# S5's rotation table built per group of four, with priority for the gates' weight splits and the late adaLN steps behind S5's steps

## The chip, the core and the metric

One core of a Trainium2 chip. The metric is the device time of one execution in microseconds (us), as the median of the runs shown. The engines are TensorE (PE, matmuls), VectorE (DVE), ScalarE (ACT), GpSimd (POOL) and SyncE (SP), whose queue issues most DMAs.

## The reference, cut to what matters

```python
mod = jax.nn.silu(c) @ w_ada + b_ada                       # six vectors of 1024
h = layer_norm(x) * (1.0 + scale1) + shift1                # 1024 x 1024
z = h @ w_in
zq, zkv, zg, zs, zm = jnp.split(z, splits, axis=-1)        # zm: 2048 columns, zs: 512
o_a = nsa_attention(...)                                   # from zq, zkv, zg
y_s = s5_ssm(zs, ...)                                      # 32 groups x 64 states, complex
zz = jax.nn.gelu(y_s) @ w_s5_glu
y_b = zz[..., :d] * jax.nn.sigmoid(zz[..., d:])
g_a, g_b = jnp.split(zm, 2, axis=-1)
mix = (jax.nn.sigmoid(g_a) * (o_a @ w_nsa_out) + jax.nn.sigmoid(g_b) * y_b) @ w_o
x = layer_norm(alpha * x + gate1 * mix) * ln1_g + ln1_b    # then a gated MLP with a conv
```

The S5 mixer is a scan over 1024 positions with the state multiplied by a complex number at each step. The kernel cuts the sequence into 128 blocks of 8 positions. Between blocks it needs the complex rotation e^(i·angle·c) for c = 0 to 127: this is the table E, which is built by doubling (the first n columns times the rotation of n blocks give the next n).

## The kernel before

Order of the stages: layer norm of x and the first two adaLN vectors; the S5 input `zs` (matmuls `pz`) and S5's parameters (`s5_params`); then sixteen gates `zm` of 128 columns each with S5 beside them; then keys, values and queries, attention, the merge and the MLP. Each weight is split into a high and a low part, and a product is three matmuls (`mm3`: high·high, low·high, high·low).

**A gate** (`z_gate`, zm0 to zm15) is 48 matmuls of 128x512. Its weight comes through the class `Stream`: a DMA on SP loads `wr` (512 KB, three buffers), ACT makes `wh` from it (L112), DVE (POOL from the tenth gate on) the remainder `wl` (L113). The first matmul of a gate needs `wh`, the third `wl`. `wl` frees the `wr` buffer for a later load.

**Late adaLN steps.** After each gate stand two steps (`late`, `ada_acc`) that add one more 128 rows of w_ada, scaled, to an accumulator `acc` (DVE L263 for the first, L265 for the others). They take `wr` buffers from the same three, so SP's queue holds in turn one gate weight and two such loads, in order. I call the steps l0, l1, l2 and so on: l0 and l1 belong to zm0.

**S5** (`s5_steps`, a generator) goes through four groups of four states, q4 = 0 to 3, in three pieces each, one piece for each `next(s5)`, which stands at the end of `z_gate`:
- POOL makes the products `s5V` and `s5W` of the group (14 instructions, L589 to L608), DVE copies `s5V` into `s5VB` (L617);
- PE makes `s5pk`, `s5pu`, `s5pw` (8 matmuls each), DVE and ACT write them out; `s5kt` goes to memory and comes back as `s5T`;
- PE makes `s5pb`, ACT copies it to `s5B`, and DVE runs a chain of 27 instructions on it and on E: six on `s5r` (L668 to L673), eight scans `s5S` (L677), four multiplications (L681 to L684) and four that give `s5X` (L688, L689). PE's `s5py` needs `s5X`.

Engines work in order; a scheduler fixes the order from the program's order and priorities. E of before is built in `s5_params` in two halves of eight states, with its real and imaginary part in separate tiles; the first half lies in the tile `bias`, which the attention's bias needs later (L906 to L911 on POOL write it).

Of the kernel before, what the change touches and what calls it, by code (L numbers as in the profile page):

```python
# [33 lines left out]
def kernel(  # L34
# [6 lines left out]
    V, A, G, TE, SP = nc.vector, nc.scalar, nc.gpsimd, nc.tensor, nc.sync  # L41
# [12 lines left out]
    def Bt(shape, dt=F32, name="b"):  # L54
        return sp.tile(shape, dt, name=name, tag="B", bufs=20)
# [13 lines left out]
    bc = lambda a, shape: a.to_broadcast(list(shape))  # L69


    class Stream:
# [20 lines left out]
        def split(self, upto):  # L93
            while self.ns < min(upto, len(self.specs)):
                i = self.ns
                _, shape, eng, dest, raw_only, scale = self.specs[i]
                self.load(i + 1)
                r = self.raw.pop(i)
                self.ns += 1
                if raw_only:  # L100
                    self.hl[i] = r
                    continue
                if callable(dest):
                    h, l = dest()
                elif dest is None:
                    h = sp.tile([P] + list(shape), F32R, name="wh", tag="wh", bufs=2)
                    l = sp.tile([P] + list(shape), F32R, name="wl", tag="wl", bufs=2)
                else:
                    h, l = Bt([P] + list(shape), F32R, "bh"), Bt([P] + list(shape), F32R, "bl")
                if scale is not None:  # L110
                    (V if eng is G else G).tensor_mul(r, r, self.scales[scale])  # L111
                A.activation(h, r, AF.Copy)  # L112
                (eng or G).tensor_sub(l, r, h.bitcast(F32))  # L113
                self.hl[i] = (h, l)

        def get(self, i, ahead=3, split=2):
# [2 lines left out]
            self.split(i + split)  # L119
            return self.hl.pop(i)  # L120

    W = Stream()

    def colw(w, ncols, c0, n, k0=0, nk=8):
        return ap(w, k0 * P * ncols + c0, [ncols, P], [P * ncols, nk], [1, n])
# [16 lines left out]
    for i in range(NT):  # L142
        t = (Bt if i < 4 else Ct)([P, 1024], name="x")
# [23 lines left out]
    ORDER = [("z", m) for m in range(16)] + [(t[0], int(t[1])) for t in "r0 r1 k0 c0 k1 c1 q0 C0 q1 C1 q2 n0 q3 n1".split()]  # L167
    for kind, n in ORDER:
        if kind == "z":
            zm_i[n] = W.add([(None, colw(w_in, IN_COLS, C_ZM + P * n, P))], [8, P], eng=V if n < 10 else G)  # L170
            for v, k in lateada[2 * n:2 * n + 2]:
                late_i[v, k] = W.add([(None, ada_src(v, k))], [1024], raw_only=True)
        elif kind == "r":
            kc_i[n] = W.add([(None, colw(w_in, IN_COLS, (C_KC, C_VC)[n], P))], [8, P], eng=V)
        elif kind == "n":
            for kk, (k0, nk) in enumerate(((0, 3), (3, 3), (6, 2))):
                nat_i[n, kk] = W.add([((slice(None), slice(0, nk), slice(0, 128)), colw(w_in, IN_COLS, C_VS, 128, k0, nk)),
                                      ((slice(None), slice(0, nk), slice(128, 280)), colw(w_in, IN_COLS, C_VW, 152, k0, nk))],
                                     [nk, 280], eng=V)
# [182 lines left out]
    bias_t = lambda: sp.tile([P, 2176], F32, name="bias", tag="bias", bufs=1)  # L362

    def s5_params():
# [9 lines left out]
        bbt = Bt([P, 4, 16, 16], name="s5bb")  # L374
# [7 lines left out]
        p = ps(name="s5p")  # L382
        TE.transpose(p[:, 0:36], rows2, ident[0:36, 0:36])
        prm = cst.tile([P, 36], F32, name="s5prm")
        V.tensor_copy(prm, p[:, 0:36])
        p = ps(name="s5c")
# [3 lines left out]
        CT = Bt([P, 3, 16, 16], name="s5CT")  # L390
# [34 lines left out]
        cs, sn = tab[:, 320:480], tab[:, 480:640]  # L425
        nn, q, z, r2, a1, a2 = (wk[:, k] for k in range(6))
# [39 lines left out]
        for d, n in ((2, 1), (4, 3)):  # L466
            br, bi = (bc(L[:, a, d:d + 1], [P, n, 16]) for a in range(2))
# [6 lines left out]
        LT = Bt([P, 2, 16, 17], name="s5LT")  # L474
        for a in range(2):
            V.tensor_copy(LT[:, a, :, 0:9], L[:, a].rearrange("p d q -> p q d"))
            for j in range(8):
# [24 lines left out]
        G.tensor_tensor(tmp, bbt[:, 2], cib, op=OP.mult)  # L502
        G.tensor_tensor(bbt[:, 1], bbt[:, 1], tmp, op=OP.add)

        et = bias_t()
        E = [[et[:, 1024 * a:1024 * a + 1024].rearrange("p (q c) -> p q c", q=8) for a in range(2)],
             [Bt([P, 8, 128], name="s5E") for _ in range(2)]]
        for qh in range(2):
            er, ei = E[qh]
            V.memset(er[:, :, 0:1], 1.0)  # L510
            V.memset(ei[:, :, 0:1], 0.0)
            u1 = Bt([P, 8, 64], name="s5u1")
            u2 = Bt([P, 8, 64], name="s5u2")
            for k in range(7):
                n = 1 << k
                c0 = 16 * (3 + k) + 8 * qh
                br, bi = (bc(t[:, c0:c0 + 8][:, :, None], [P, 8, n]) for t in (cs, sn))
                V.tensor_tensor(u1[:, :, :n], er[:, :, 0:n], br, op=OP.mult)
                V.tensor_tensor(u2[:, :, :n], ei[:, :, 0:n], bi, op=OP.mult)
                V.tensor_tensor(er[:, :, n:2 * n], u1[:, :, :n], u2[:, :, :n], op=OP.subtract)  # L520
                V.tensor_tensor(u1[:, :, :n], er[:, :, 0:n], bi, op=OP.mult)
                V.tensor_tensor(u2[:, :, :n], ei[:, :, 0:n], br, op=OP.mult)
                V.tensor_tensor(ei[:, :, n:2 * n], u1[:, :, :n], u2[:, :, :n], op=OP.add)
        BZ = Bt([P, 2, 4, P], name="s5BZ")
        G.memset(BZ, 0.0)
        VB = Bt([P, 2, 4, P], name="s5VB")
# [3 lines left out]
            V.tensor_add(dmask, dmask, ident[:, 16 * m:16 * m + 16])  # L530
        m8 = cst.tile([P, 16], F32, name="s5m8")
        V.tensor_copy(m8, mg[:, 48:64])
        return dict(CT=CT, LT=LT, bb=bbt, E=E, BZ=BZ, VB=VB, m8=m8, dmask=dmask, Dc=prm[:, 32:36])

    kd_d = dp.tile([32, 16, 240], F32, name="kd_d")
    ys_d = dp.tile([P, 4, 1024], F32, name="ys_d")
# [45 lines left out]
    def s5_steps():  # L582
        S = S5
        for q4 in range(4):
# [30 lines left out]
            for a in range(2):  # L615
                for g2 in range(2):
                    V.tensor_copy(S["VB"][64 * a:64 * a + 64, g2], Vt[a][64 * g2:64 * g2 + 64].rearrange("p s d h -> p s (d h)"))  # L617
            yield
            pk = ps((P, P), name="s5pk")
            n = 0  # L620
# [38 lines left out]
            for g2 in range(2):  # L659
                for a in range(2):  # L660
                    A.activation(Bv[64 * g2:64 * g2 + 64, a],
                                 pb[g2][64 * a:64 * a + 64].rearrange("p (s c) -> p s c", s=4), AF.Copy)
            e0, e1 = (t[:, q0 % 8:q0 % 8 + 4] for t in S["E"][q4 // 2])
            N1 = slice(0, 127)
            N2 = slice(1, 128)
            r0 = Bt([P, 2, 4, P], name="s5r0")
# [71 lines left out]
    def z_gate(m):  # L738
        wh, wl = W.get(zm_i[m])
        p = mm("zm")  # L740
        gemmT(p, wh, wl, hH, hL, KD)
        sg = Bt([P, 1024], name="sg")
        A.activation(sg, p, AF.Tanh, scale=0.5)
        A.dma_start(zm_d[m], sg)
        for v, k in lateada[2 * m:2 * m + 2]:
            late(v, k)
        next(s5, None)


    vcs = cst.tile([P, 2, P], F32R, name="vcs")  # L750
# [854 lines left out]
```

## Time and profile before

| what | value |
|---|---|
| runs | 1692.97, 1693.41, 1701.58 us; median 1693.41 us |
| the profiled execution | 1698.03 us, its span 1696.3 us |
| PE busy in the span | 1569.0 us (92%) |
| DVE, POOL, ACT busy | 1239.6, 706.2, 691.1 us |
| TensorE clock granted, mean | 0.969 |
| first matmul of zm0 / zm2 / zm3 / zm8 | 97.1 / 123.4 / 152.7 / 232.9 us |

Times within the rows are microseconds from the start of the span. The busy time of an engine says how full it is over the whole span; what a stage costs is read from the idle time of PE in that stage, which is shown in square brackets together with what ended it.

### The profile page before, as it was taken

The page shows a single profiled execution, that of the slowest core. Times are in us where ns is not written, and L with a number is a line of the kernel's source. Part 1 is how long each engine was busy: PE and PEld are TensorE (multiplying, and loading weights), DVE is VectorE, ACT ScalarE, POOL GpSimd, SP SyncE. Part 2 cuts the span into 40 slices and gives each one's busy share as a digit, 9 for nine tenths or more (in the row PEclk, how much of TensorE's full clock was granted, in tenths as well). Part 3 has the DMA queues.
Part 4 walks back from the last instruction along what each step waited for, and adds up shares of the span by engine and source line. Part 5 has one row for each costly group of instructions (what it writes and reads, how often), then busy time and mean ns, then how long its engine had stood idle before and what let it go on. Part 6 is the DMA issues. An engine that isn't in the chain of part 4 may idle for free.

```text
span 1696.3 us, 21512 instructions
## 1 busy us (share of the span) xinstructions
PE 1569.0 (92%) x7707; PEld 1304.0 (77%) x7707; DVE 1239.6 (73%) x2263; ACT 691.1 (41%) x1303; POOL 706.2 (42%) x584
## 2 busy tenths in 40 slices
PE   6987899999999999999998579999999998899996
PEld 4976787878989999788787357777777776688885
DVE  8699766565399999553658876888888888855448
ACT  4423223224399999421323433444344333311101
POOL 4342355400066566222536634544444555521105
PEclk8998999999999999999999789999999999999998
DMA  9235544622200010443411112222222227522102
GB/s 341 70 113 151 167 146 152 202 64 79 71 20 1 14 38 2 145 132 123 137 62 63 38 50 87 75 75 75 75 75 75 75 88 251 208 100 99 39 2 99
DMA packets 150128, 164.36 MB, mean 97 GB/s; under 512 B 20633, under 2 KB 123777, under 8 KB 150021
## 3 DMA queue, kind: packets, MB, share of 16 engines
q1 hardware_dynamic: 146357, 151.74, 27.9%
q10 hardware_dynamic: 3664, 11.24, 1.7%
q8 instruction: 61, 1.00, 0.2%
q14 instruction: 46, 0.38, 0.1%
HBM read 132.04 MB, written 30.91 MB: 96 GB/s over the span
## 4 chain that ended last, share of the span: by engine, by line
PE 57%; DVE 27%; issue 6%; ACT 5%; POOL 2%; DMA 2%; SPq 0%; DVEq 0%; ACTq 0%; POOLq 0%
DVE cv L1382 5%; PE dn L1472 4%; PE dn L1474 4%; PE dn L1473 4%; PE oacc L1008 3%; PE pT L1019 3%; PE up L1346 3%; PE up L1348 2%; PE up L1347 2%; DVE us L1321 2%; PE zm L128 2%; PE zm L130 2%; ACT cv L1379 2%; PE zm L129 2%; DVE us L1306 2%
## 5 line engine op out<-in xcount | busy, mean ns | idle before, releaser
L982 POOL TENSOR_SCALAR Pm<-Pm,gate,fc 128x64 f32<-128x64 f32 (+4 forms) x192 | 123.8, 659 | 57.3 <-DVE fc L980 56.8
L1472 PE MATMUL dn<-dnh,fh 128*128 128x512 f32 x320 | 124.9, 390 | 4.5 <-DVE facc L1570 4.5
L1296 POOL TENSOR_TENSOR ul<-wr,uh 128x512 fp32r<-128x512 f32 x44 | 77.7, 1785 | 115.4 <-ACT uh L1295 115.4
L1474 PE MATMUL dn<-dnh,fl 128*128 128x512 f32 x320 | 124.1, 389 | 1.6 <-DVE fl L1463 1.6
L1570 DVE SCALAR_TENSOR_TENSOR facc<-facc,dn 128x512 f32<-128x512 f32 x96 | 64.7, 681 | 83.3 <-PE dn L1474 83.3
L1473 PE MATMUL dn<-dnl,fh 128*128 128x512 f32 x320 | 124.5, 389 | 0.0
L978 ACT ACTIVATE Pm<-Pm,ng 128x64 f32<-128x64 f32 (+6 forms) x192 | 114.7, 602 | 6.5 <-DVE ng L959 5.0
L130 PE MATMUL zm<-hTh,wl 128*128 128x512 f32 x256 | 101.8, 398 | 13.1 <-DVE wl L113 13.1
L112 ACT ACTIVATE wh<-wr 128x1024 fp32r<-128x1024 f32 (+3 forms) x59 | 57.7, 978 | 137.8 <-PE ya L129 30.6
L111 POOL TENSOR_TENSOR wr<-wr,g2b 128x1024 f32<-128x1024 f32 x22 | 63.3, 2885 | 120.5 <-DMA wr<-in_w_down_dram 79.4
L1023 DVE TENSOR_TENSOR Pt<-pT,Pt 128x512 fp32r<-128x512 f32 (+1 forms) x160 | 100.6, 642 | 9.7 <-ACT Pt L1022 8.7
L128 PE MATMUL zm<-hTh,wh 128*128 128x512 f32 x256 | 101.9, 398 | 2.9 <-ACT wh L112 2.5
L1008 PE MATMUL oacc<-Pt,Vs 128*128 128x256 f32 x528 | 102.6, 304 | 0.9 <-DVE Pt L1023 0.4
L129 PE MATMUL zm<-hTl,wh 128*128 128x512 f32 x256 | 101.2, 395 | 0.0
L113 DVE TENSOR_TENSOR wl<-wr,wh 128x1024 fp32r<-128x1024 f32 (+2 forms) x40 | 51.8, 1294 | 64.4 <-ACT wh L112 64.2
L1019 PE MATMUL pT<-ident,Pm 128*128 128x128 f32 x592 | 91.3, 273 | 1.9 <-DVE yl L1082 1.0
L1379 ACT ACTIVATE cv<-u,cw 128x512 f32<-128x512 f32 x44 | 35.6, 809 | 140.3 <-DVE u L1369 132.7
L1022 ACT ACTIVATE Pt<-pT 128x512 fp32r<-128x512 f32 (+1 forms) x160 | 87.4, 560 | 13.1 <-PE pT L1019 12.1
L1382 DVE SCALAR_TENSOR_TENSOR cv<-u,cw,cv 128x511 f32<-128x511 f32 x88 | 74.8, 851 | 19.7 <-ACT cv L1379 18.8
L1347 PE MATMUL up<-h2b,uh 128*128 128x512 f32 (+1 forms) x184 | 72.2, 393 | 15.1 <-POOL h2b L1199 15.1
L1346 PE MATMUL up<-h2b,uh 128*128 128x512 f32 (+1 forms) x184 | 74.4, 406 | 12.1 <-DVE bias L1355 9.0
L1323 POOL TENSOR_TENSOR ul<-us,uh 128x1024 fp32r<-128x1024 f32 x22 | 52.8, 2398 | 74.8 <-ACT uh L1322 71.2
(507 smaller groups left out, 4871.0 us busy)
## 6 DMA issues: line engine op xcount, KB each, us to landing
wr<-in_w_up_dram SPq DMA_DIRECT2D x44, 512.0 KB, 3.8
wr<-in_w_in_dram SPq DMA_DIRECT2D x32, 512.0 KB, 4.2
wr<-in_w_ada_dram SPq DMA_DIRECT2D x32, 512.0 KB, 4.1
ff_d<-cv SPq DMA_DIRECT2D x22, 512.0 KB, 2.8
wr<-in_w_down_dram SPq DMA_DIRECT2D x22, 512.0 KB, 4.0
fl<-ff_d SPq DMA_DIRECT2D x22, 512.0 KB, 6.0
ar<-in_w_ada_dram SPq DMA_DIRECT2D x16, 512.0 KB, 9.4
zm_d<-sg ACTq DMA_DIRECT2D x16, 512.0 KB, 2.9
```

The costliest lines, as they stand in the source:

```text
L128: TE.matmul(po, wh, rh, start=start, stop=False, skip_group_check=skip)
L129: TE.matmul(po, wh, rl, start=False, stop=False, skip_group_check=skip)
L130: TE.matmul(po, wl, rh, start=False, stop=stop, skip_group_check=skip)
L978: A.activation(Pm[ii][:, c0:c0 + n], Pm[ii][:, c0:c0 + n], AF.Exp, bias=ng[:, ii, br:br + 1], scale=-1.0, accum_out=dn[:, ii, br:br + 1])
L982: G.tensor_scalar(Pm[ii][:, c0:c0 + n], Pm[ii][:, c0:c0 + n], gate[:, i, 3 * h + br:3 * h + br + 1], fc[:, ii, br:br + 1], op0=OP.mult, op ...
L1008: TE.matmul(acc[:, a0:a0 + 256], vt, ptile[:, hl, 256 * w:256 * w + 256], start=(first and n == 1), stop=(last and n == nmm), skip_group_c ...
L1019: TE.transpose(p[:, o:o + P], Pm[e][:, c0:c0 + P], ident)
L1346: TE.matmul(po, wh[:, q], h, start=(q == 0 and j not in (3, 4, 7)), stop=False, skip_group_check=True)
L1382: V.scalar_tensor_tensor(dst[:, c0:c0 + n], src[:, 0:n], tap(d), dst[:, c0:c0 + n], op0=OP.mult, op1=OP.add)
L1472: TE.matmul(p, ff[0][:, c0], wd[0][:, s], start=(e == 0), stop=False)
L1473: TE.matmul(p, ff[0][:, c0], wd[1][:, s], start=False, stop=False)
L1474: TE.matmul(p, ff[1][:, c0], wd[0][:, s], start=False, stop=(e == len(fs) - 1))
```

## The change

E is built by `make_E(q4)` once for each group of four, from within that group's first piece of `s5_steps`. Real and imaginary part lie in one tile, so that one multiplication takes both with the cosine and one both with the sine: four instructions per doubling instead of six per half of eight. `bias` is no longer used for it. The split of a gate's weight (`wh`, `wl`) runs under the scheduler's high priority. In `z_gate` the S5 piece is now ahead of the two late steps.

```diff
@@ Stream.split
-                A.activation(h, r, AF.Copy)
-                (eng or G).tensor_sub(l, r, h.bitcast(F32))
+                with tc.high_priority() if i in urgent else ExitStack():
+                    A.activation(h, r, AF.Copy)
+                    (eng or G).tensor_sub(l, r, h.bitcast(F32))
@@ ORDER, for a gate
+            urgent.add(len(W.specs))
             zm_i[n] = W.add(...)
@@ s5_params
-        et = bias_t()
-        E = [[et[:, 1024 * a:1024 * a + 1024].rearrange("p (q c) -> p q c", q=8) for a in range(2)],
-             [Bt([P, 8, 128], name="s5E") for _ in range(2)]]
-        for qh in range(2):
-            er, ei = E[qh]
-            V.memset(er[:, :, 0:1], 1.0)
-            V.memset(ei[:, :, 0:1], 0.0)
-            u1 = Bt([P, 8, 64], name="s5u1")
-            u2 = Bt([P, 8, 64], name="s5u2")
+        def make_E(q4):
+            t = Bt([P, 2, 4, 128], name="s5E")
+            V.memset(t[:, 0, :, 0:1], 1.0)
+            V.memset(t[:, 1, :, 0:1], 0.0)
+            uu = Bt([P, 2, 2, 4, 64], name="s5u")
             for k in range(7):
                 n = 1 << k
-                c0 = 16 * (3 + k) + 8 * qh
-                br, bi = (bc(t[:, c0:c0 + 8][:, :, None], [P, 8, n]) for t in (cs, sn))
-                V.tensor_tensor(u1[:, :, :n], er[:, :, 0:n], br, op=OP.mult)
-                V.tensor_tensor(u2[:, :, :n], ei[:, :, 0:n], bi, op=OP.mult)
-                V.tensor_tensor(er[:, :, n:2 * n], u1[:, :, :n], u2[:, :, :n], op=OP.subtract)
-                V.tensor_tensor(u1[:, :, :n], er[:, :, 0:n], bi, op=OP.mult)
-                V.tensor_tensor(u2[:, :, :n], ei[:, :, 0:n], br, op=OP.mult)
-                V.tensor_tensor(ei[:, :, n:2 * n], u1[:, :, :n], u2[:, :, :n], op=OP.add)
+                c0 = 16 * (3 + k) + 4 * q4
+                for i, a in enumerate((cs, sn)):
+                    V.tensor_tensor(uu[:, i, :, :, :n], t[:, :, :, 0:n], bc(a[:, None, c0:c0 + 4, None], [P, 2, 4, n]),
+                                    op=OP.mult)
+                V.tensor_tensor(t[:, 0, :, n:2 * n], uu[:, 0, 0, :, :n], uu[:, 1, 1, :, :n], op=OP.subtract)
+                V.tensor_tensor(t[:, 1, :, n:2 * n], uu[:, 1, 0, :, :n], uu[:, 0, 1, :, :n], op=OP.add)
+            return t
@@ s5_steps, after the copies into s5VB
+            E = S["make_E"](q4)
             yield
@@ z_gate
+        next(s5, None)
         for v, k in lateada[2 * m:2 * m + 2]:
             late(v, k)
-        next(s5, None)
```

What the scheduler makes of it stands in the order of the instructions. Lines of the changed kernel are three higher from L263 on (L263 becomes L266, L265 becomes L268) and one higher from about L500 on. First DVE, from the last S5 parameters on, with zm1 running on PE. Before:

```order
L518 TENSOR_TENSOR s5u_787<-bias,s5tab 128x8
L519 TENSOR_TENSOR s5u_788<-bias,s5tab 128x8
L510 MEMSET s5E 128x8
L511 MEMSET s5E 128x8
L520 TENSOR_TENSOR bias<-s5u_787,s5u_788 128x8
L518 TENSOR_TENSOR s5u_833<-s5E,s5tab 128x8
L519 TENSOR_TENSOR s5u_834<-s5E,s5tab 128x8
L263 TENSOR_SCALAR acc<-wr,scol 128x1024
```

and after the change, at the same place:

```order
L617 COPY s5VB<-s5V 64x512 x2
L511 MEMSET s5E 128x4
L512 MEMSET s5E 128x4
L518 TENSOR_TENSOR s5u<-s5E,s5tab 128x8 x2
L266 TENSOR_SCALAR acc<-wr,scol 128x1024
L520 TENSOR_TENSOR s5E<-s5u 128x4
L521 TENSOR_TENSOR s5E<-s5u 128x4
L628 MEMSET s5kt 128x112
L268 SCALAR_TENSOR_TENSOR acc<-wr,scol,acc 128x1024
```

The first pair of copies into `s5VB`, which stood some fifty rows further down, is now ahead of E's first instructions and of l0 (L266) and l1 (the first L268).

PE, from the end of zm1 on. Before, zm2 begins at once (its first rows are not shown), and S5's products of q4 = 0 are strewn over its 48 matmuls; this is where they begin:

```order
L128 MATMUL zm<-hTh,wh 128x512
L623 MATMUL s5pk<-s5V,s5BZ 128x128
L641 MATMUL s5pu<-ident,uc 128x128 x8
L129 MATMUL zm<-hTl,wh 128x512
L130 MATMUL zm<-hTh,wl 128x512
L128 MATMUL zm<-hTh,wh 128x512
L129 MATMUL zm<-hTl,wh 128x512
L623 MATMUL s5pk<-s5V,s5BZ 128x128 x7
```

After, from the last matmul of zm1 to the first of zm2:

```order
L132 MATMUL zm<-hTh,wl 128x512
L624 MATMUL s5pk<-s5V,s5BZ 128x128
L642 MATMUL s5pu<-ident,uc 128x128 x8
L624 MATMUL s5pk<-s5V,s5BZ 128x128 x7
L649 MATMUL s5pw<-ident,s5W 128x2x64 x8
L130 MATMUL zm<-hTh,wh 128x512
```

All 24 products of q4 = 0 now stand between zm1 and zm2. In the same way q4 = 0's `s5pb` stands ahead of zm3 (before: seven matmuls into it), and all its `s5py` ahead of zm4 (before: after 42 of zm4's matmuls).

POOL, between the products of q4 = 1 and of q4 = 2. Before:

```order
L608 TENSOR_TENSOR s5W<-s5W,s5tA 128x512
L906 IOTA bias 128x1024
L907 IOTA bias 128x640
L908 IOTA bias 128x512
L910 TENSOR_SCALAR bias<-bias 128x2176
L911 AFFINE_SELECT bias<-bias 128x1024
L911 AFFINE_SELECT bias<-bias 128x640
L911 AFFINE_SELECT bias<-bias 128x512
L911 AFFINE_SELECT bias<-bias 128x640
L589 COPY s5V<-s5CT 128x4x16
L590 TENSOR_SCALAR s5V<-s5CT 128x4x16
```

After:

```order
L608 TENSOR_TENSOR s5W<-s5W,s5tA 128x512
L589 COPY s5V<-s5CT 128x4x16
L590 TENSOR_SCALAR s5V<-s5CT 128x4x16
L594 TENSOR_TENSOR s5V<-s5CT,s5LT 128x4x128
```

The eight instructions that prepare the attention's bias have left this place; they now stand at the start of the program, right behind the identity matrix and ahead of POOL's share of the layer norm of x.

## Rows read from the trace of the kernel before

**Rows 1.** PE, idle between zm2 and zm5: start, duration, instruction, idle before it and what ended it.

```profile
123.42 0.50 PE L128 MATMUL zm<-hTh,wh 128*128 128x512 f32 x1 [2.48 <-ACT wh L112]
...
135.81 0.79 PE L130 MATMUL zm<-hTh,wl 128*128 128x512 f32 x1 [11.66 <-DVE wl L113]
...
184.80 0.80 PE L701 MATMUL s5py<-s5VB,s5X 128*128 128x128 f32 x2 [7.47 <-DVE s5X L689]
```

**Rows 2.** Windows of PE: stretch, length, busy (instructions), granted clock, DMA share, GB/s.

```profile
110.00:120.00 10.00, 10.00 (x46) 1.00 0.37 119
135.80:142.00 6.20, 6.19 (x20) 0.53 0.76 187
185.00:192.00 7.00, 7.00 (x36) 0.69 0.59 179
```

**Rows 3.** DVE beside zm1's end and zm2: start, duration, instruction.

```profile
114.40 1.13 DVE L263 TENSOR_SCALAR acc<-wr,scol 128x1024 f32<-128x1024 f32 x1
...
115.77 2.17 DVE L265 SCALAR_TENSOR_TENSOR acc<-wr,scol,acc 128x1024 f32<-128x1024 f32 x1
117.86 1.03 DVE L523 TENSOR_TENSOR bias<-s5u,s5u 128x8 f32<-128x8 f32 x1
...
137.28 0.84 DVE L617 COPY s5VB<-s5V 64x512 f32<-64x512 f32 x2
```

**Rows 4.** DVE at the start of the program.

```profile
3.53 0.58 DVE L530 TENSOR_TENSOR s5dm<-s5dm,ident 128x16 f32<-128x16 f32 x3
5.59 1.29 DVE L240 BATCH_NORM_STATS2 bn<-x 128x6 f32<-128x512 f32 x2 [1.47 <-DMA x<-in_x_dram]
```

**Rows 5.** POOL, products of q4 = 0.

```profile
116.82 2.04 POOL L595 TENSOR_TENSOR s5tA<-s5CT,s5LT 128x512 f32<-128x512 f32 x1
118.82 1.07 POOL L597 TENSOR_TENSOR s5V<-s5CT,s5LT 128x512 f32<-128x512 f32 x1
...
123.48 1.27 POOL L596 TENSOR_TENSOR s5V<-s5V,s5tA 128x512 f32<-128x512 f32 x1
...
132.58 1.30 POOL L608 TENSOR_TENSOR s5W<-s5W,s5tA 128x512 f32<-128x512 f32 x1
```

**Rows 6.** SP, the issue of zm2's load.

```profile
117.97 0.38 SPq L89 DMA_DIRECT2D wr<-in_w_in_dram  x1
```

**Rows 7.** ACT, zm2's wh.

```profile
122.31 1.06 ACT L112 ACTIVATE wh<-wr 128x1024 fp32r<-128x1024 f32 x1 [5.50 <-DMA wr<-in_w_in_dram]
```

**Rows 8.** DVE's chain of q4 = 1, then PE's first product with its s5X.

```profile
221.31 0.69 DVE L668 TENSOR_TENSOR s5r<-s5B,bias 128x508 f32<-128x508 f32 x1 [2.00 <-ACT s5B L661]
...
224.90 1.69 DVE L677 TENSOR_TENSOR_SCAN s5S<-s5m,s5r 128x127 f32<-128x127 f32 x5
...
231.22 1.40 DVE L689 TENSOR_TENSOR s5X<-s5r 64x508 f32<-64x508 f32 x2
...
231.96 0.49 PE L701 MATMUL s5py<-s5VB,s5X 128*128 128x128 f32 x2
```

**Rows 9.** DVE's chain of q4 = 0 from the scans on, then POOL's first product of q4 = 1.

```profile
165.80 3.31 DVE L677 TENSOR_TENSOR_SCAN s5S<-s5m,s5r 128x127 f32<-128x127 f32 x5
...
174.73 2.08 DVE L113 TENSOR_TENSOR wl<-wr,wh 128x1024 fp32r<-128x1024 f32 x1
...
183.12 2.35 DVE L689 TENSOR_TENSOR s5X<-s5r 64x508 f32<-64x508 f32 x2
...
164.74 1.50 POOL L589 COPY s5V<-s5CT 128x64 f32<-128x64 f32 x1 [30.86 <-DVE s5E L523]
```

**Rows 10.** POOL, the preparation of bias, then the products of q4 = 2.

```profile
229.98 0.98 POOL L906 IOTA bias<- 128x1024 f32 x1 [45.77 <-DVE s5r L683]
...
232.22 2.28 POOL L910 TENSOR_SCALAR bias<-bias 128x2176 f32<-128x2176 f32 x1
234.57 5.29 POOL L911 TENSOR_SCALAR_AFFINE_SELECT bias<-bias 128x1024 f32<-128x1024 f32 x4
239.82 1.21 POOL L589 COPY s5V<-s5CT 128x64 f32<-128x64 f32 x1
```

More of the change, by code (lines that the diff above doesn't have):

```diff
@@ L120, in get @@
             return self.hl.pop(i)
+    urgent = set()
     W = Stream()
@@ L532, in s5_params @@
         V.tensor_copy(m8, mg[:, 48:64])
-        return dict(CT=CT, LT=LT, bb=bbt, E=E, BZ=BZ, VB=VB, m8=m8, dmask=dmask, Dc=prm[:, 32:36])
+        return dict(CT=CT, LT=LT, bb=bbt, make_E=make_E, BZ=BZ, VB=VB, m8=m8, dmask=dmask, Dc=prm[:, 32:36])
     kd_d = dp.tile([32, 16, 240], F32, name="kd_d")
@@ L662, in s5_steps @@
                                  pb[g2][64 * a:64 * a + 64].rearrange("p (s c) -> p s c", s=4), AF.Copy)
-            e0, e1 = (t[:, q0 % 8:q0 % 8 + 4] for t in S["E"][q4 // 2])
+            e0, e1 = E[:, 0], E[:, 1]
             N1 = slice(0, 127)
```

## The prediction

> **What bounds the kernel now.** The table of busy times comes first: PE has by far the most work, so time is won or lost where PE stands still or runs at its lower clock. I then went through PE's own rows for idle time in the stretch that the change touches, from zm0 to the end of the gates. Three places hold nearly all of it [rows 1]. zm2 starts after 2.48 us without work, because its `wh` was late; two matmuls on, PE waits 11.66 us for `wl`; and in zm4 it waits 7.47 us for `s5X` of q4 = 0. The reader should then look at the windows [rows 2]: behind the first two waits PE works 6.20 us at a granted clock of 0.53, behind the third 7.00 us at 0.69, against 1.00 beside zm1. [...] So 21.6 us of waits and 5.1 us of clock are there to be won, 26.7 us or 1.6% of 1693 us. Everything else from zm0 on is PE at work, so whatever the change wins or loses here goes through to the end nearly one to one.
>
> Why is `wl` of zm2 late? DVE's rows of that time [rows 3] show one instruction of 8 elements that takes 1.03 us, where three of 16 elements took 0.58 us together at the start [rows 4]: POOL is at its products then, and DVE's small instructions wait for it. `wl` stands behind E's instructions in DVE's order. Priority for `wl` removes that. The question is what PE waits for next.
>
> **zm2 (one term).** DVE's order after the change puts the first copies into `s5VB` ahead of E and of l0 and l1. These copies need POOL's L596, which in the trace ends at 123.48 + 1.27 = 124.75 [rows 5]. DVE is through with the parameters just ahead of l0's 114.40, so it now stands still for some nine us. POOL has the time for itself: a product that took 2.04 us takes 1.07 us alone [rows 5], two such are found ahead of L596, and I take 122.8 for its end. Then come the copies (0.84 us), four small instructions, l0 and l1. From l0's start to l1's end before took 114.40 to 117.94, 3.5 us, with three small ones between [rows 3]; I put l1's end at 123.6 + 1.0 + 3.5 to 4, or 128.5, ten us later than before. The issue of zm2's load at 117.97 follows l1's end at once [rows 6], since l1 frees its buffer. It landed in time for `wh` at 122.31, 4.3 us later [rows 7]. So after the change `wr` is there at about 133, where it was needed at 121.
>
> Two more things stand ahead of zm2's first matmul. On PE all 24 products of q4 = 0 now come first, and the last of them need POOL's L608, which ended at 133.88 [rows 5], with the seven `s5pw` behind it. On ACT `wh` stands behind the two issues of `kd_d`, which need `s5kt` of DVE, which needs `s5pk`. With POOL's end at 131 to 135, then `s5pk`, `s5kt`, the two issues and 1.06 us of `wh` [rows 7], zm2 starts at 134 to 139; I take 137.3. `wl` has priority and follows in DVE's order one instruction group later: 1.2 us more. The big wait is thus not removed; it changes its cause.
>
> What is won is that S5's products are out of the way. Before, from 135.81 to the start of zm3 at 152.7, PE did 45 matmuls of zm2 and these 24. 46 matmuls fit in 10.00 us at full clock [rows 2], so 45 are some 10.1 us; with 2.9 us for the clock 3.9 us remain for the 24. After: 137.3 + 10.7 (48 matmuls) + 1.2 (`wl`) + 2.9 (clock, since PE stands still as before) = 152.1. (`s5pb`, now ahead of zm3 and before just inside it, costs the same on either side and is left out.) So the term is 152.1 - 152.7 = **-0.6 us**, with -5 (134, no `wl` wait) and +2 (139) as its ends.
>
> **`s5py` of q4 = 0 (second term).** Both sides move. PE asks for `s5X` ahead of zm4, 42 matmuls earlier than before. It asked at 184.80 - 7.47 = 177.3; now at 152.1 + 10.7 and the products of `s5pb` and the first of `s5py`, about 166. `s5X` comes earlier too: E is four groups instead of two halves, so only 28 multiplications and additions and two memsets stand ahead of the first chain instead of 84 and four, and before the last one of E stood inside the chain. What does the chain take? Beside an idle POOL (q4 = 1) it went from 221.31 to 232.62, 11.3 us, of which 7.7 us from the scans on [rows 8]. Beside POOL's products (q4 = 0) the part from the scans on went from 165.80 to 185.47; without the 2.08 us of a `wl` in it, that is 17.6 us [rows 9]: 9.9 us more for the same instructions. It now starts when `s5B` is written, at about 159. POOL's products of q4 = 1 began before only at 164.74, after E's last instruction [rows 9]; that wait is gone, and no row tells how far they then lie beside the chain. Alone, `s5X` is there at 170, beside POOL throughout at 180 or later. The wait is 4 to 14 us, and I take 7.5, near the lower third, since POOL may start early: **0 us**, from -3 to +7. The clock behind it costs as before.
>
> **`s5py` of q4 = 1 (third term, and the one that decides).** Before, PE's first product with `s5X` stands at 231.96, while DVE makes the last pair of `s5X` from 231.22 on [rows 8]: no wait, but no slack either. POOL did nothing beside that chain until 229.98 [rows 10], because the preparation of `bias` waited for the last read of E in it (idle 45.77 us), and q4 = 2's products stood behind that preparation and began at 239.82 [rows 10]. After the change neither wait is there: q4 = 2's products follow q4 = 1's directly, and fall beside the chain or before it. Their price is 0 if they are done or held elsewhere, up to 9.9 us if they lie beside all of it. I take half, 4.5 us of new wait, and 1.9 us of clock behind it, somewhat less than the 2.2 us of a wait of 7.47: **+6.4 us**, ends 0 and +12.
>
> [...]
>
> **The start (fourth term).** The preparation of `bias`, 229.98 to 239.86, so 9.9 us [rows 10], moves to POOL's start, where POOL is idle from about 2 to 17 us before the normalisation of x. It hides there, except from DVE: the last additions into `s5dm` end at 4.11, and `bn_stats` follow at 5.59 [rows 4]. An addition that waits for POOL's longest single instruction, the 2.28 us at 232.22 [rows 10], and a short one behind it delay them by at most 2.7 us, and the start is a chain from DVE to PE. **+0.8 us**, 0 to 2.7. Without POOL's idle time the whole 9.9 us would show.
>
> E costs nothing of its own in q4 = 1 to 3: DVE sits idle between the gates there (2.00 us ahead of the chain alone [rows 8]). If that cover is gone, it comes as a later `s5X`, within the ends above.
>
> **Sum.** -0.6 + 0 + 6.4 + 0.8 = +6.6 us, against 1698.03 us of the profiled execution, which is 4.6 us above the median; I carry the difference to the median and take off half a us for small waits that go: 1693.4 + 6 = **1699 us**, 0.35% slower. A measurement of this kernel tells about 0.5%, 8.5 us, from no change.
>
> **The rivals.**
> *Faster.* POOL, undisturbed, ends early, zm2 starts at 134 and q4 = 1's chain finds POOL done. For it: DVE is idle for nine us while POOL works. Against it: L608 and `kd_d` stay ahead of zm2. -5 - 3 + 0 + 0.8 = -7.2, and with shorter low-clock stretches -9: 1684 us. All three waits gone would be 1667 us; PE's order, with POOL's last products ahead of zm2, speaks against that.
> *Slower.* POOL's products lie beside both chains. It decides if they start after about 155 for q4 = 1 and after 215 for q4 = 2. The part from the scans on then takes 17.6 us instead of 7.7: +10 and 2 of clock at q4 = 1, +3 at q4 = 0, -0.6 and +0.8: +15, or 1708 us. [...]
> *The change does nothing* but exchange one wait for another, with q4 = 1 hidden: 1693 us.
>
> **Chances.** The forecast with the exchange (1686 to 1702): 0.52. Slower: 0.31. Faster: 0.17. The range from 1684 to 1709 reaches to both other cases.
>
> **What would show it.** PE's idle time ahead of zm2, by `s5pk`, `s5pw` or `wh` instead of `wl`, 12 to 16 us; zm3 within 3 us of 152.7; a wait for `s5X` of 4 to 14 us ahead of zm4; a new wait for `s5X` ahead of zm8 and POOL at L594 to L608 beside that chain; `bn_stats` under 3 us later. I am wrong if zm2 starts before 130, or if q4 = 1's chain stays at 11 us.

## The result, and the profile after

The changed kernel takes 1706.39 us in the median of 7 runs (1705.64 to 1708.08), the kernel before, on the same chips, 1699.3 us (7 runs, 1692.97 to 1701.58). The ratio is 1.0052, 95% interval 1.0034 to 1.0069: slower by 7.1 us, where 6 were forecast. The time itself lies 7.4 us above the 1699 of the forecast, because that stood on the 1693.41 us of the first three runs of before.

Where the time went is read best from the first matmul of a gate; kc is the first matmul behind the gates, after which both kernels do the same. Microseconds from the start of the span:

| kernel | zm0 | zm2 | zm3 | zm5 | zm7 | zm9 | zm12 | zm13 | kc |
|---|---|---|---|---|---|---|---|---|---|
| before | 97.1 | 123.4 | 152.7 | 191.6 | 217.0 | 246.1 | 286.6 | 301.9 | 342.4 |
| after | 97.1 | 136.4 | 152.0 | 190.5 | 216.0 | 251.5 | 292.0 | 310.0 | 350.4 |
| after - before | 0 | +13.0 | -0.7 | -1.1 | -1.0 | +5.4 | +5.4 | +8.1 | +8.0 |

So up to zm7 the two are even, 6.4 us are lost between zm7 and zm9, 2.7 between zm12 and zm13, and nothing else up to kc. PE's idle times of the changed kernel say by what (start, duration, instruction, idle before it and what ended it):

```profile
125.36 1.83 PE L624 MATMUL s5pk<-s5V,s5BZ 128*128 128x128 f32 x14 [1.87 <-POOL s5V L599]
129.46 0.33 PE L649 MATMUL s5pw<-ident,s5W 128*128 128x128 f32 x1 [2.27 <-POOL s5W L605]
...
134.17 1.73 PE L649 MATMUL s5pw<-ident,s5W 128*128 128x128 f32 x7 [4.38 <-DVE s5kt L630]
136.35 0.79 PE L130 MATMUL zm<-hTh,wh 128*128 128x512 f32 x1 [0.46 <-ACT wh L113]
...
138.16 0.80 PE L132 MATMUL zm<-hTh,wl 128*128 128x512 f32 x1 [0.59 <-DVE wl L114]
...
174.37 0.79 PE L702 MATMUL s5py<-s5VB,s5X 128*128 128x128 f32 x2 [8.26 <-DVE s5X L690]
...
235.08 0.80 PE L702 MATMUL s5py<-s5VB,s5X 128*128 128x128 f32 x2 [4.12 <-DVE s5X L690]
...
299.76 0.49 PE L702 MATMUL s5py<-s5VB,s5X 128*128 128x128 f32 x2 [0.88 <-DVE s5X L690]
...
301.23 0.60 PE L702 MATMUL s5py<-s5VB,s5X 128*128 128x128 f32 x2 [0.76 <-DVE s5X L690]
```

These answer to [rows 1]. The 11.66 us for `wl` are gone, but in their place PE waits in pieces for POOL (1.87, 2.27), 4.38 for `s5kt` and about a us for `wh` and `wl`. The wait for `s5X` of q4 = 0 is there still, 8.26 instead of 7.47. New are 4.12 us for `s5X` of q4 = 1 at 235.08, and 0.88 + 0.76 where before 0.75 stood, for `s5X` of q4 = 2. (This chain runs from 284.43 to 301.17 and is the third of the four, so q4 = 2; the expectations below call its wait that of q4 = 3.) The clock in the windows behind the three (stretch, length, busy, granted clock, DMA share, GB/s):

```profile
174.30:181.00 6.70, 6.63 (x35) 0.68 0.28 80
235.00:242.00 7.00, 6.92 (x30) 0.64 0.29 89
302.00:306.00 4.00, 4.00 (x24) 0.64 0.24 38
```

In the kernel before, the clock stayed up behind the single wait of 0.75 us for q4 = 2:

```profile
298.00:302.00 4.00, 4.00 (x24) 1.00 0.65 164
```

Behind each wait of the changed kernel the mean granted clock was 0.64 to 0.68. Microsecond by microsecond it was 0.50 at first and 1.00 in the end (behind the wait of q4 = 1, 0.50 in each of the five from 235.00 on, then 0.99 and 1.00), and the 128x512 matmuls there start 0.43 us apart at 0.50 (237.38, 237.81) and 0.23 us apart at 0.99 (240.22, 240.45). By that pace the cost is estimated as the stretch times what the clock lacks to 1.00: 6.70 x 0.32 = 2.1 us at q4 = 0, as before (7.00 x 0.31 = 2.2 us, which with 6.20 x 0.47 = 2.9 us at zm2 makes the prediction's 5.1 us [rows 2]), and as new costs 7.00 x 0.36 = 2.5 us at q4 = 1 and 4.00 x 0.36 = 1.4 us at q4 = 2. 4.12 + 2.5 is about the loss between zm7 and zm9; 0.9 more idle time and 1.4 of clock are most of that behind zm12.

How zm2 came to be late shows first in DVE's timeline of the changed kernel:

```profile
122.03 2.14 DVE L617 COPY s5VB<-s5V 64x512 f32<-64x512 f32 x2 [8.01 <-POOL s5V L596]
...
125.33 0.74 DVE L266 TENSOR_SCALAR acc<-wr,scol 128x1024 f32<-128x1024 f32 x1
...
127.13 1.16 DVE L268 SCALAR_TENSOR_TENSOR acc<-wr,scol,acc 128x1024 f32<-128x1024 f32 x1
...
133.80 0.22 DVE L630 SCALAR_TENSOR_TENSOR s5kt<-s5dm,s5prm,s5pk 128x16 f32<-128x16 f32 x1
```

DVE stands idle for 8.01 us until POOL has L596, as the order said, and l1 ends at 128.29. SP's timeline has zm2's load right behind it ([rows 6]: 117.97):

```profile
128.31 0.38 SPq L89 DMA_DIRECT2D wr<-in_w_in_dram  x1
```

And ACT's timeline shows `kd_d`, which waits for the `s5kt` of 134.02, ahead of zm2's `wh`:

```profile
134.05 1.14 ACTq L633 DMA_DIRECT2D kd_d<-s5kt  x2
135.24 1.06 ACT L113 ACTIVATE wh<-wr 128x1024 fp32r<-128x1024 f32 x1 [6.01 <-DVE acc L268]
```

The `acc` (L268) that the profile names here had been done since 128.29; what ACT came through last was `kd_d`.

The chain of q4 = 1 in DVE's timeline:

```profile
220.25 0.69 DVE L669 TENSOR_TENSOR s5r<-s5B,s5E 128x508 f32<-128x508 f32 x1 [2.00 <-ACT s5B L662]
...
222.69 1.55 DVE L671 TENSOR_TENSOR s5r<-s5r 128x508 f32<-128x508 f32 x1
...
225.63 2.56 DVE L678 TENSOR_TENSOR_SCAN s5S<-s5m,s5r 128x127 f32<-128x127 f32 x5
...
231.42 2.14 DVE L689 TENSOR_TENSOR s5X<-s5r 64x508 f32<-64x508 f32 x2
233.59 3.10 DVE L690 TENSOR_TENSOR s5X<-s5r 64x508 f32<-64x508 f32 x2
```

and POOL's products of q4 = 2 beside it:

```profile
225.12 1.51 POOL L597 TENSOR_TENSOR s5V<-s5CT,s5LT 128x512 f32<-128x512 f32 x1
231.65 1.37 POOL L603 TENSOR_TENSOR s5W<-s5bb,s5LT 128x512 f32<-128x512 f32 x1 [5.02 <-DVE s5r L684]
```

The chain goes from 220.25 to 236.69, 16.4 us instead of 11.3 [rows 8]. POOL's first three big products stand beside its first half, where an `s5r` product takes 1.55 instead of 0.69 us. Then POOL waits 5.02 us until a product of the chain (`s5r`, L684) is done, and starts again just beside `s5X`: the last two pairs take 2.14 and 3.10 us instead of 1.4 each.

### The profile page after: what moved, and what is told of

Same layout as the page of the kernel before. It is cut to its first block, busy times and chain, and to the rows that moved or that the text cites. A ratio compares the mean times of both kernels' runs of the same rounds, so it can differ in the third digit from the quotient of the medians.

```text
span 1706.4 us, 21547 instructions
## 1 busy us (share of the span) xinstructions
PE 1575.6 (92%) x7707; PEld 1310.4 (77%) x7707; DVE 1241.3 (73%) x2295; ACT 690.7 (40%) x1303; POOL 700.8 (41%) x584
## 4 chain that ended last, share of the span: by engine, by line
PE 54%; DVE 22%; issue 5%; ACT 4%; POOL 1%; DMA 1%; SPq 0%; ACTq 0%; DVEq 0%; POOLq 0%
DVE cv L1383 5%; PE dn L1473 4%; PE dn L1474 4%; PE dn L1475 4%; PE oacc L1009 3%; PE up L1347 3%; PE pT L1020 3%; PE up L1349 3%; PE up L1348 2%; DVE us L1322 2%; DVE us L1307 2%; ACT cv L1380 2%; PE zm L130 1%; PE zm L131 1%; PE zm L132 1%
## 5 line engine op out<-in xcount | busy, mean ns | idle before, releaser
L114 POOL TENSOR_TENSOR wl<-wr,wh 128x1024 fp32r<-128x1024 f32 (+1 forms) x19 | 37.5, 1974 | 122.7 <-ACT wh L113 121.5
```

## The experiments

Ten kernels ran: the first four, up to q2mem, on one chip, the next four on a second, the last two on a third, each group beside the kernel before. Gate times are read from one profiled execution of each kernel.

**The parts of the change, each alone.** First the table, as an edit of the changed kernel:

```diff
-                with tc.high_priority() if i in urgent else ExitStack():
-                    A.activation(h, r, AF.Copy)
-                    (eng or G).tensor_sub(l, r, h.bitcast(F32))
+                A.activation(h, r, AF.Copy)
+                (eng or G).tensor_sub(l, r, h.bitcast(F32))
...
-        next(s5, None)
         for v, k in lateada[2 * m:2 * m + 2]:
             late(v, k)
+        next(s5, None)
```

> Of the three parts only the table E per group of four; the splits have no priority and the late steps stand ahead of S5's step, as before. Theory A (the loss comes from two places: the late steps behind S5's step put the copies into s5VB, which wait for POOL, ahead of l0 and l1 and so of zm2's load and products; and the freed bias lets q4 = 2's products run beside q4 = 1's chain): zm2's load is issued near 118 again, wh ends PE's wait near 123 and wl follows within about 2 us, since a third of E's instructions is ahead of it; zm3 starts near 146 instead of 152, the wait for s5X ahead of q4 = 0's s5py falls under 3 us, and a wait of 3 to 4 us for s5X of q4 = 1 stays, one gate earlier than in the changed kernel. Sum: about 12 us faster than the kernel before, 18 to 20 faster than the changed one. Rival B (E within a group's step lengthens the way to s5X in each group): the waits for s5X stay as in the changed kernel, 12 us or more in all, and the time is that of the changed kernel or above.

Measured: 1686.2 us against 1697.94, ratio 0.9936 (0.9911 to 0.9961), 11.7 us faster; zm3 at 145.7, zm5 at 176.9, kc at 333.2. PE's waits:

```profile
123.67 0.50 PE L129 MATMUL zm<-hTh,wh 128*128 128x512 f32 x1 [1.83 <-ACT wh L112]
...
125.45 0.79 PE L131 MATMUL zm<-hTh,wl 128*128 128x512 f32 x1 [1.05 <-DVE wl L113]
...
142.90 0.63 PE L648 MATMUL s5pw<-ident,s5W 128*128 128x128 f32 x4 [2.37 <-DVE s5kt L629]
...
219.99 0.49 PE L701 MATMUL s5py<-s5VB,s5X 128*128 128x128 f32 x2 [2.57 <-DVE s5X L689]
```

zm2's `wh` and `wl` come as in theory A, and q4 = 1's wait is there, 2.57 us. No wait for q4 = 0's `s5X` of more than a us is left. E is then not ahead of `wl` at all, where theory A had left a third of it: DVE's order has it behind l0 to l3 and zm2's `wl`. Rival B falls.

The order of the late steps alone, as an edit of the kernel before:

```diff
+        next(s5, None)
         for v, k in lateada[2 * m:2 * m + 2]:
             late(v, k)
-        next(s5, None)
```

> Of the three parts only the order in z_gate: S5's step ahead of the two late steps; E in two halves as before. Theory A: l0 and l1 go behind the copies into s5VB, zm2's load is issued ten us or more later, and all 24 products of q4 = 0 stand ahead of zm2, which starts near 145; zm3 10 us later than before; the later s5X wait shrinks to 4 us in all; q4 = 1 has no wait, since bias still holds q4 = 2's products back. Sum: 5 to 9 us slower than the kernel before. Rival C (the order is harmless, and E or the priority costs the time): within 3 us of before.

Measured: 1704.44 us against 1697.94, ratio 1.0043 (1.0026 to 1.006), 6.5 us slower; zm2 at 145.5, zm3 at 161.8, kc at 349.9. The longest wait of PE, and its two for q4 = 2:

```profile
144.03 1.08 PE L648 MATMUL s5pw<-ident,s5W 128*128 128x128 f32 x4 [12.40 <-DVE s5kt L629]
...
299.17 0.49 PE L701 MATMUL s5py<-s5VB,s5X 128*128 128x128 f32 x2 [0.88 <-DVE s5X L689]
...
300.63 0.49 PE L701 MATMUL s5py<-s5VB,s5X 128*128 128x128 f32 x2 [0.76 <-DVE s5X L689]
```

Size and place are as expected, the middle link is not: l0 ran at 136.85, and what held it was not the copies, which took 0.84 us at 135.97 and had no wait for POOL any more, but most of E ahead of them, which this kernel builds in halves of eight. PE's wait was for `s5kt`, which stood on DVE behind l1 and l2. q4 = 1 has no wait, as expected. The two waits for q4 = 2 are those of the changed kernel, and zm12 to zm13 takes 18.0 us in both, against 15.3 before. Rival C's first half (the order is harmless) falls.

The priority alone, as an edit of the kernel before:

```diff
-                A.activation(h, r, AF.Copy)
-                (eng or G).tensor_sub(l, r, h.bitcast(F32))
+                with tc.high_priority() if i in urgent else ExitStack():
+                    A.activation(h, r, AF.Copy)
+                    (eng or G).tensor_sub(l, r, h.bitcast(F32))
```

> Of the three parts only the priority for the gates' splits. Theory A: wl of zm2 stays behind E's instructions, which come first in the program; the same waits as before at zm2 (2.5 and 11.7 us) and q4 = 0 (7.5 us), the time within 2 us of before. Rival C (the priority takes ACT and DVE from S5's chain): s5X waits grow by 3 us or more; or, if the priority works as its name says, the 11.7 us at zm2 are gone.

Measured: 1698.82 against 1697.94 us, ratio 0.9999 (0.9987 to 1.0012): no difference. The wait it might have ended:

```profile
136.49 0.80 PE L132 MATMUL zm<-hTh,wl 128*128 128x512 f32 x1 [11.53 <-DVE wl L114]
```

11.53 us for `wl`, where 11.66 stood [rows 1]. The wait for `s5X` of q4 = 0 is 9.03 instead of 7.47 us, but from zm0 to kc the two are even (245.8 and 245.3 us). The priority alone neither moves `wl` ahead of E nor costs anything that shows in the time.

**POOL's products of q4 = 2 left out.** Three memsets stand for the twelve big products of that group, whose part of the output is then left out; an edit of the changed kernel:

```diff
+            if q4 == 2:
+                G.memset(Vt[0], 0.0)
+                G.memset(Vt[1], 0.0)
+            else:
...
+            if q4 == 2:
+                G.memset(Wt, 0.0)
+            else:
```

> The changed kernel, with POOL's twelve products of q4 = 2 left out: the three tiles are filled by a memset each, so S5's third group gets zeros. POOL then only writes beside q4 = 1's chain. Theory A: the chain of q4 = 1 takes 11 to 12 us again, the wait of 4.1 us for its s5X ahead of zm8 and the low clock behind it are gone, zm9 starts near 245 instead of 251.5; 6 us less than the changed kernel, or 8 if the small wait of q4 = 3 goes with it. Rival B (E's own instructions make s5X late): the wait at zm8 stays at 4 us and the time within 2 us of the changed kernel.

Measured: 1695.56 against 1697.94 us, ratio 0.9986 (0.9973 to 1.0), where the changed kernel has 1.0052. DVE's timeline in q4 = 1, the last two `s5r` products and the pairs of `s5X`:

```profile
225.08 0.67 DVE L678 TENSOR_TENSOR s5r<-s5r 128x508 f32<-128x508 f32 x1
225.68 0.67 DVE L681 TENSOR_TENSOR s5r<-s5r 128x508 f32<-128x508 f32 x1
...
231.20 1.37 DVE L696 TENSOR_TENSOR s5X<-s5r 64x508 f32<-64x508 f32 x2
232.60 1.40 DVE L697 TENSOR_TENSOR s5X<-s5r 64x508 f32<-64x508 f32 x2
```

and POOL's timeline, with the memsets beside the `s5r` products:

```profile
225.26 0.96 POOL L608 MEMSET s5W<- 128x1024 f32 x1 [0.32 <-issue]
```

The chain goes from 222.63 to 234.00, 11.4 us; between 150 and 345 PE has one wait left, the 8.6 us of q4 = 0. From zm0 to zm9 the kernel takes 247.5 - 98.6 = 148.9 us, against 154.4 for the changed kernel and 149.0 for the one before. The wait of q4 = 1 is POOL's products, shown; rival B falls. The two small waits of q4 = 2 went as well, and from zm0 to kc it is 9.3 us less than the changed kernel, a little more than the 8 us of the expectation; but POOL had less to do later too, so this run doesn't say what ended those waits.

**The changed kernel without its late steps' order.**

```diff
-        next(s5, None)
         for v, k in lateada[2 * m:2 * m + 2]:
             late(v, k)
+        next(s5, None)
```

> The changed kernel with the late steps back ahead of S5's step: E per group and the priority stay. Theory A (the order of the late steps is the whole harm, the priority does nothing): the time of E per group alone, 0.6 to 0.7% faster than before, zm3 near 146, the wait for s5X of q4 = 1 at 2 to 3.5 us. Rival C (the priority has a part in the loss when E is per group): more than 3 us slower than E per group alone.

Measured: 1687.16 against 1697.05 us, ratio 0.9951 (0.9932 to 0.997); zm3 at 144.5, kc at 331.3, 2 us earlier than with E alone, 1.2 us if both are counted from zm0. The gain of 0.5% is a little less than the 0.6 to 0.7% expected; the intervals of the two kernels overlap, and the stage in question isn't longer. q4 = 1's wait is 2.57 us, as expected. Rival C falls. The small wait of q4 = 2 is a single one of 0.75 us here, as before, and zm12 to zm13 takes 15.3 us. So the order of the late steps makes the difference between 0.995 and 1.005.

**The copies into `s5VB` on ACT**, as an edit of the changed kernel:

```diff
-                    V.tensor_copy(S["VB"][64 * a:64 * a + 64, g2], Vt[a][...].rearrange(...))
+                    A.activation(S["VB"][64 * a:64 * a + 64, g2], Vt[a][...].rearrange(...), AF.Copy)
```

> The changed kernel with the four copies into s5VB of each group on ACT instead of DVE. Theory A (the copies, which wait for POOL, hold up DVE's queue, and with it l0, l1, s5kt and E): l0 and l1 run near 114 to 117 again although they stand behind S5's step, s5kt is no longer late, the 4.4 us ahead of s5pw go, zm2 starts 2 to 3 us earlier only, since all of q4 = 0's products stay ahead of it, but E is done ten us earlier and the 8.3 us for s5X of q4 = 0 shrink to under 3; zm5 near 180 instead of 190; 6 to 10 us faster than the changed kernel. Rival D (the late steps are late because they stand behind E, or because of SP's order, not because of the copies): zm5 and the time within 3 us of the changed kernel.

Measured: 1693.34 against 1697.05 us, ratio 0.9988 (0.9976 to 1.0), so 0.64% below the changed kernel's 1.0052, some 11 us. l0 and l1 in DVE's timeline:

```profile
115.55 0.82 DVE L266 TENSOR_SCALAR acc<-wr,scol 128x1024 f32<-128x1024 f32 x1
...
117.30 2.09 DVE L268 SCALAR_TENSOR_TENSOR acc<-wr,scol,acc 128x1024 f32<-128x1024 f32 x1
```

and PE's waits:

```profile
126.20 0.80 PE L624 MATMUL s5pk<-s5V,s5BZ 128*128 128x128 f32 x2 [4.35 <-POOL s5V L596]
...
136.39 0.80 PE L130 MATMUL zm<-hTh,wh 128*128 128x512 f32 x1 [2.87 <-ACT wh L113]
...
170.77 0.49 PE L702 MATMUL s5py<-s5VB,s5X 128*128 128x128 f32 x2 [0.96 <-DVE s5X L690]
```

l0 and l1 are back where they were, with the late steps still behind S5's; zm2 starts at 136.4, as in the changed kernel, held by POOL and ACT now; the wait of q4 = 0 is 0.96 instead of 8.26 us and zm5 is at 179.9 instead of 190.5. From zm0 to kc it takes 239.8 us against 253.3. That the copies hold up DVE's queue is shown, and rival D falls. Three points of theory A are off: zm2 gains nothing instead of 2 to 3 us, the whole is more than 6 to 10 us, and the link to q4 = 0 isn't E, which ends at 145.3 here and at 145.0 in the changed kernel. What makes that wait is read further down.

**Towards a faster kernel.** Three edits on top of E alone. POOL is held until the chain of the group before is done (the tiles `tA` and `Wt` are made earlier for it, not shown):

```diff
+            if q4 in (1, 2):
+                for t in (Vd[0][:, 0, 1, 0:1], Vd[1][:, 0, 1, 0:1], tA[:, 0, 0, 0:1], Wt[:, 0, 0, 0, 0:1], Wt[:, 1, 0, 0, 0:1]):
+                    G.tensor_copy(t, S["X"][:, 0, 0, 126:127])
```

> E per group alone, and POOL held back: five copies of one element of the last group's s5X into the tiles of the products stand ahead of the products of q4 = 1 and q4 = 2, so these begin only when the chain before is done. Theory A: the 2.6 us for s5X of q4 = 1 go, and so does what is left of a wait at q4 = 0; the chain of q4 = 1 takes 11 to 12 us; 2 to 4 us faster than E per group alone, about 0.85% faster than before. Rival E (a held POOL makes the next group's s5pk late): new waits for POOL of 3 us or more, no gain.

Measured: 1685.77 against 1697.05 us, ratio 0.9935 (0.9915 to 0.9956). DVE's timeline in q4 = 1, the first and the last row of the chain:

```profile
205.92 0.69 DVE L671 TENSOR_TENSOR s5r<-s5B,s5E 128x508 f32<-128x508 f32 x1 [2.23 <-ACT s5B L664]
...
215.84 1.40 DVE L692 TENSOR_TENSOR s5X<-s5r 64x508 f32<-64x508 f32 x2
```

POOL's timeline, where it was released:

```profile
216.65 0.76 POOL L592 COPY s5V<-s5X 128x1 f32<-128x1 f32 x2 [32.81 <-DVE s5X L692]
```

and a new wait of PE:

```profile
312.96 0.30 PE L651 MATMUL s5pw<-ident,s5W 128*128 128x128 f32 x1 [2.77 <-DVE s5kt L632]
```

The chain takes 11.3 us again (205.92 to 217.24), the wait of q4 = 1 is gone, and zm9 comes at 230.8 instead of 235.7. But later PE waits 2.77 us for `s5kt` of q4 = 3 (1.01 in E alone), and kc is at 332.3 instead of 333.2. Theory A is right on the chain and wrong on the sum, 0.9 instead of 2 to 4 us; rival E has its wait, though smaller and by way of DVE.

Then the remainders `wl` of zm10 to zm12, which POOL makes otherwise, go to DVE:

```diff
-            zm_i[n] = W.add(..., eng=V if n < 10 else G)
+            zm_i[n] = W.add(..., eng=V if n < 13 else G)
```

> As the run before, and the remainders wl of zm10 to zm12 on DVE instead of POOL, so that POOL has less to do beside q4 = 3's chain. Theory A (every wait for s5X is POOL's work beside the chain): the wait of q4 = 3 (0.8 to 3 us, with a low clock behind it) goes as well; about 8 us faster than E per group alone, 1.1 to 1.2% faster than before. Rival F (q4 = 3's chain is late for DVE's own load): the wait stays or grows, since DVE has three more instructions of 1.2 us.

Measured: 1682.89 against 1697.05 us, ratio 0.9922 (0.9906 to 0.9938); kc at 326.0, and no wait for `s5X` of 0.6 us or more in any group. The chain of q4 = 2 takes 13.5 us instead of 17.8 with the hold alone. Rival F falls; the expected 1.1 to 1.2% is not reached. Without the hold:

> E per group alone and the remainders wl of zm10 to zm12 on DVE; POOL is not held back. It tells what in the fastest kernel so far comes from which of its two additions. Theory A (each wait for s5X has its own work of POOL beside it): the 2.6 us of q4 = 1 come back, with a low clock behind them, the wait of q4 = 3 stays gone; 4 to 5 us slower than with POOL held back, 5 to 7 faster than E per group alone, about 0.95% faster than before. Rival G (the hold gains nothing, as in the run with the hold alone, and all comes from the remainders): the same time as with both, within 2 us.

Measured: 1686.76 against 1696.88 us, ratio 0.9933 (0.9911 to 0.9956); kc at 329.6. PE's wait in q4 = 1 is back, the later ones stay gone:

```profile
218.72 0.49 PE L701 MATMUL s5py<-s5VB,s5X 128*128 128x128 f32 x2 [2.76 <-DVE s5X L689]
```

From zm0 to kc it takes 232.5 us, 4.4 more than with the hold, and 2.7 less than E alone. Theory A holds for the hold, rival G falls; against E alone the remainders by themselves are worth less than the 5 to 7 us. The two edits bring 0.9 and 2.7 us alone and 7.1 together. The medians alone would not have told it: the two kernels with the remainders on DVE differ by 4 us, with overlapping intervals. And with the priority:

> The fastest kernel so far (E per group, POOL held back, three remainders on DVE) with the priority for the gates' splits as well: two of the change's three parts. Theory A (the priority is worth nothing once E is out of wl's way): within 2 us of the same without it, 0.75 to 0.95% faster than before, no wait for s5X in any group. Rival C: 3 us or more slower.

Measured: 1678.89 against 1696.88 us, ratio 0.989 (0.987 to 0.991), 18 us faster than before, with one wait of 0.63 us for `s5X` left: the fastest run of the study, and 1.6% below the changed kernel. From zm0 to kc it takes 230.1 us, against 228.1 without the priority, so that its ratio is below 0.9922 doesn't come from the gates. Rival C (3 us or more slower) falls; theory A's 2 us hold for the gates, while the gain of 1.1% is more than it said.

## Why the prediction was right

**The number.** 1706.39 us lies above the forecast's own band of 1686 to 1702, close to the 1708 of the slower case, and within the whole range. The band stood on 1693.4 us; from 1699.3 the forecast is 1705.3. That it was the forecast's case and not the slower one is seen from the mechanism: POOL's products lie beside about half of q4 = 1's chain, and the wait is 4.12 us, not 10. That 6 and 7.1 us lie so close is in part luck. The gates lost 8.0 us, of which 2.7 had no term; the 0.8 us of the start did not come; and the medians differ by less than the gates do.

**zm2 (-0.6 us forecast, -0.7 at zm3).** The parts: L596 ended at 121.99 (122.8 taken), l1 at 128.29 (128.5), zm2 started at 136.4 (137.3). The load and `wh` came as worked out. Not foreseen as PE's own wait were the 4.38 us for `s5kt`: the second tile of `s5pw` takes the PSUM buffer of `s5pk` (the kernel has four for these tiles, in turn), which is free when `s5kt` has been read out. It led to the same time, since `wh` hung on the same `s5kt` through `kd_d`. PE's idle time ahead of zm2 is 1.87 + 2.27 + 4.38 + 0.46 = 9.0 us, less than the 12 to 16 given as a sign. The claim was that gain and loss cancel: S5's 24 products out of zm2, against a start 13 us later. They nearly did, but the agreement to 0.1 us is luck. The prediction left `s5pb` out, and in the changed kernel it stands ahead of zm3's first matmul:

```profile
150.09 1.95 PE L657 MATMUL s5pb<-s5U,s5Wx 128*128 128x128 f32 x16
```

Without it zm2's own matmuls end at 150.1, 2.6 us ahead of 152.7, within the range of -5 to +2. One reading was off as well: 46 matmuls and not 45 remained of zm2 behind its wait, and the 10.1 and 10.7 us for 45 and 48 matmuls don't follow from 46 in 10.00 us, which gives 9.8 and 10.4. Both change the term by less than half a us.

**q4 = 0 (0 forecast, -0.4 between zm3 and zm5).** With `s5pb` counted on the same side as before it is +1.5, within the range of -3 to +7; the two terms together came to -1.1 us against -0.6. The wait is 8.26 us (7.5 taken, 7.47 before). The chain started at 159.76 (159). It ran beside POOL in its scans and at the end, and alone in between, because POOL waited 3.67 us until an `s5r` product of the chain was done. That is why the middle was the right choice; the prediction's reason for it, that POOL may start early, was another.

Why the chain starts so late is read on SP, ACT and DVE of the changed kernel:

```profile
153.19 0.38 SPq L89 DMA_DIRECT2D wr<-in_w_in_dram  x1
...
156.97 1.06 ACT L113 ACTIVATE wh<-wr 128x1024 fp32r<-128x1024 f32 x1 [4.15 <-DMA wr<-in_w_in_dram]
157.93 2.42 ACT L662 ACTIVATE s5B<-s5pb 64x512 f32<-64x512 f32 x4
...
159.76 0.69 DVE L669 TENSOR_TENSOR s5r<-s5B,s5E 128x508 f32<-128x508 f32 x1 [0.48 <-ACT s5B L662]
```

and on ACT of the kernel with the copies on ACT (s5vb_on_act):

```profile
151.20 2.44 ACT L662 ACTIVATE s5B<-s5pb 64x512 f32<-64x512 f32 x4 [0.54 <-PE s5pb L657]
```

In both, PE is through with `s5pb` by about 152 (152.0 and 151.4). In the changed kernel `s5B` stands on ACT behind zm4's `wh`, which waits 4.15 us for a load issued at 153.19; with the copies on ACT that load is issued at 147.46, `s5B` comes ahead of `wh`, and the chain starts at 153.13. So the copies' wait reaches q4 = 0 through late loads and ACT; DVE itself was waiting for `s5B`, with E done. It is not the whole of the difference: `s5py` also stands 20 matmuls further into zm4 in that kernel, so PE asks later.

**q4 = 1 (+6.4 forecast, +6.4 measured).** 4.12 us of wait and 2.5 of clock, against 4.5 and 1.9. q2mem shows the cause, e_hold confirms it on another kernel. The mechanism was forecast; the half was a choice between two ends, and that it came out so closely is luck. Not all work of POOL costs the chain: in q2mem POOL's memset of `s5W` (0.96 us from 225.26) lies beside two `s5r` products that take 0.67 us each, no more than the 0.69 of such a product alone [rows 8], and the same two take 1.55 us each beside POOL's big products in the changed kernel. The term stayed at half of its range, which ends at 12 us, since POOL was held midway (5.02 us, until L684).

**The start (+0.8 forecast, 0.0).** The range (0 to 2.7) was right and the choice too high. The last additions took 2.30 us beside POOL's `bias` (L911, 2.00 us from 3.87 on) instead of 0.58 [rows 4], but `bn_stats` slipped by 0.23 us only ([rows 4]: 5.59), and zm0 starts at 97.1 in both:

```profile
3.60 2.30 DVE L530 TENSOR_TENSOR s5dm<-s5dm,ident 128x16 f32<-128x16 f32 x3
5.82 1.27 DVE L243 BATCH_NORM_STATS2 bn<-x 128x6 f32<-128x512 f32 x2
```

**Missed: q4 = 2 (+2.7 us).** The prediction gave no term for it. The wait grew from 0.75 to 1.64 us, and behind it the granted clock was 0.64 in the mean of 4.00 us, where it was 1.00 before. The chain itself is no longer than before (16.8 us against 17.1) and starts 7.6 us ahead of zm12 in both. But PE asks earlier: the first `s5py` that needs `s5X` stands behind 29 matmuls of zm12, before behind 35. This comes with the order of the late steps: late_only has the 29 matmuls, the same two waits and the same 18.0 us from zm12 to zm13, while urgent_only, e_only and e_urgent, without that order, have 35 matmuls, a single wait of 0.75 to 0.76 and 15.3 us. e_dve and e_hold_dve show that POOL's remainders `wl` for zm10 to zm12 have a part in such a wait: with them on DVE the chain takes 13.4 to 13.5 us, and no wait is left.

**What the prediction did not see** is that its forecast was a sum of two opposite parts. E per group is worth 11.7 us alone; the order of the late steps costs 6.5 alone, where E holds up the queue, and about 17 together with E per group, where the copies do (0.9951 against 1.0052). The first term was worked out for both at once, so the gain by E and the loss by the order never appeared.

## What to carry to other kernels

Follow a step that is moved ahead to the first instruction of it that waits for another engine: everything behind it on the in-order queue gets that wait, here 8.01 us on DVE, passed on to the loads' buffers, `s5kt` and the next gate's weight, by two copies that take 0.84 us together when nothing holds them (137.28 in [rows 3]). When a buffer is freed, ask what its reuse was holding back: the preparation that waited for E had kept POOL away from DVE's chain (idle for 45.77 us [rows 10]), which took 11.3 us then and 16.4 without it. And time the parts of a change one by one; two of three parts here were worth a kernel 0.5% faster, and the third turned it into one 0.5% slower.

## What had not been expected

The time behind the gates, in which all kernels here run the same instructions but for a few, differs from run to run by as much as the effects studied. From kc to the end of the span it took 1353.9 us in the profiled run of before (1696.3 - 342.4), 1356.0 in that of the change (1706.4 - 350.4), 1346.1 in e_dve (1675.7 - 329.6) and 1357.9 in e_urgent (1689.2 - 331.3). Within one kernel it is the same: the six runs of e_dve go from 1677.39 to 1689.11 us. So effects of a few us were read here from gate to gate within the traces, and the medians used only for the rest. Why that stage varies is open.

POOL's preparation of `bias` took less at the start than in its old place: the four selections 3.01 us beside `bn_stats`, against 5.29 us [rows 10].

```profile
5.95 3.01 POOL L912 TENSOR_SCALAR_AFFINE_SELECT bias<-bias 128x1024 f32<-128x1024 f32 x4
```
